# A second token tile scored by rows of the first expert table, and gates spread by one float32 product

## The chip, the cores and the metric

The kernel runs on one core of a Trainium2 chip. The metric is the time of one execution on the device in microseconds (us), the median of several executions. The engines are TensorE (PE in the rows; PEld is its weight load), VectorE (DVE), ScalarE (ACT), GpSimd (POOL) and SyncE (SP). All DMA queues share the core's 16 DMA engines.

## The reference

One layer of a hybrid backbone for 512 tokens of width 2048. Its first half (a state space branch, a pooling branch, a merge) is not touched here. The second half is a product-key expert layer, of which this is the core:

```python
s1, s2 = q[:, :, 0] @ k1.T, q[:, :, 1] @ k2.T         # 8 heads, 128 keys each
v1, i1 = top_k(s1, 16); v2, i2 = top_k(s2, 16)
cand = v1[..., :, None] + v2[..., None, :]            # 16 x 16 pairs
top_s, pos = top_k(cand, 16)                          # 16 experts a head
eid = i1 * 128 + i2                                   # of the pairs chosen
g = softmax(top_s)
act = gelu(einsum('td,thkd->thk', hb, u_tab[eid])) * g
out = einsum('thk,thkd->td', act, v_tab[eid])
```

So each token has 8 x 16 = 128 experts of 16384, each a row of table u (16384 x 2048, float32, 134 MB) that scores it and a row of table v that is added to the output with the weight act.

## The kernel before

The tokens are four tiles of 128 (0 to 3), one token to a partition. The expert layer treats them in two ways.

**By rows.** Tile 0 (`gather_tile`, L1070 to L1110) fetches for each of its 128 experts the 128 rows of u and of v that its tokens ask for, 8 KB each, with an indirect DMA of GpSimd (L1081, 1 MB a transfer, into a pool `rows2` of three buffers). VectorE multiplies the u rows with the tokens and sums (L1096, SCALAR_TENSOR_TENSOR with an accumulator, called the u product below), ScalarE makes the weight (L1097, L1098), and VectorE adds the weighted v rows to the output tile `ffn` (L1089, the v product). A step is one expert: one u product and one v product, the latter for the expert before, then the transfers of this expert's v rows and of the next one's u rows.

**Whole.** Tiles 1 to 3 (`DT`) go through both tables with matmuls. `dense_u` (stage U) scores them against all of u: 128 blocks of 128 experts, and for each two loads of 1024 x 128 weights. `dense_gates` spreads the gates g, 128 a token, over all 16384 experts: for each token a product of two one-hot matrices, one of them weighted. The gates go to memory (`Gd`, by way of a staging tile `ast` with one buffer), the scores too (`Sd`). `dense_v` (stage V) multiplies the two (`weights`, L1193) and runs the result against all of v in 8 passes of 16 blocks, two halves each.

Every weight load, 256 in each stage, is `wload` (L114): SyncE loads 512 KB, ScalarE rounds it to `whi` (L125), and either VectorE or GpSimd makes the remainder `wlo` (L126). `lo_eng` chooses: a share `lo_pool` of them, one in two, goes to GpSimd. `mm3` (L107) then makes each product of three matmuls in rounded float32: high by high, high by low, low by high. There are three buffers of each kind.

What runs beside is spread by `lane`: a list of generators that is stepped `rate` times for each weight load (`tick`). In stage U, lane0 has tile 0's rows at 0.29 steps a load, lane1 the choice of experts (`picks`) and the gates at 1.1. In stage V lane0 goes on at 0.25. Eight blocks before the end of stage U, `late` drains lane1 and makes the first weights. Each engine works in the order in which its instructions stand. In this half GpSimd's order is that of the program, and a scheduler orders the other engines.

Of the kernel before, what the change touches and what calls it, by code (L numbers as in the profile page):

```python
# [93 lines left out]
class Builder:  # L94
# [974 lines left out]

    def gather_tile(self, t, res, acc):  # L1070

        nc, I, V, h2 = self.nc, self.I, self.nc.vector, self.h2[t]
        i1, i2, g = res[t]
        ef = self.keep.tile([P, NK], F32, name=self.nm("ef"))
        V.scalar_tensor_tensor(ef, i1, float(P), i2, op0=OP.mult, op1=OP.add)
        eid = self.keep.tile([P, NK], I32, name=self.nm("eid"))
        V.tensor_copy(eid, ef)

        def row(tab, k):
            r = self.rowp.tile([P, D], F32, tag="row", name=self.nm("row"))  # L1080
            nc.gpsimd.indirect_dma_start(out=r, out_offset=None, in_=I[tab],  # L1081
                                         in_offset=bass.IndirectOffsetOnAxis(ap=eid[:, k:k + 1], axis=0))
            return r
# [312 lines left out]
```

## Time and profile before

| | us |
|---|---|
| median of 3 runs (3973.7 to 3977.77) | 3974.51 |
| the profiled execution | 3968.97 |
| its span, first to last instruction | 3966.9 |
| TensorE busy in the span | 3750.0 (95%) |
| VectorE busy | 2561.8 (65%) |
| GpSimd busy | 1761.6 (44%) |
| ScalarE busy | 1187.9 (30%) |
| stage U, first to last matmul of `psU` | 1586 to 2850 |
| stage V, first to last matmul of `psV` | 2850 to 3947 |

The times below are of the profiled execution, counted from the span's start. A matmul's busy time overlaps its neighbours', so TensorE's pace is read from the distance of starts.

### The profile page before, as it was taken

How to read it: one execution, taken by the hardware profiler on the slowest of the kernel's cores; microseconds unless marked ns; L12 is line 12 of the kernel's file. 1: busy time of each engine (PE TensorE's matmuls, PEld its weight loads, DVE VectorE, ACT ScalarE, POOL GpSimd, SP SyncE). 2: the span in 40 equal slices, each digit the busy share in tenths (PEclk: the TensorE clock that was granted, in tenths of full speed). 3: DMA queues.
4: the chain of work that ended last, by engine and by line, in shares of the span. 5: the costliest groups of instructions: out<-in, count | busy, mean ns of one | idle time of the engine just before them, and what ended most of it. 6: DMA issues, size and time to landing. Idle time of an engine off the chain costs nothing. (4 is left out here: it accounts for less than half of the span.)

```text
span 3966.9 us, 49308 instructions
## 1 busy us (share of the span) xinstructions
PE 3750.0 (95%) x18841; PEld 3196.8 (81%) x18841; DVE 2561.8 (65%) x3331; ACT 1187.9 (30%) x1752; POOL 1761.6 (44%) x997
## 2 busy tenths in 40 slices
PE   5999998889899899899999999999999999999997
PEld 3478876667777778799999999989977887788886
DVE  4364379996563368986767767655666666665664
ACT  4223331112222222333333333323332333333332
POOL 0043115552322323354444444446555666576652
PEclk8999999999999999999999999999999999999999
DMA  8635658789875422477877778778887877887773
GB/s 269 207 124 186 206 166 231 227 227 302 235 233 175 138 70 91 136 263 281 290 272 267 288 273 291 256 289 290 312 300 279 316 285 281 287 318 282 282 277 123
DMA packets 456382, 954.40 MB, mean 241 GB/s; under 512 B 104721, under 2 KB 248465, under 8 KB 421073
## 3 DMA queue, kind: packets, MB, share of 16 engines
q1 hardware_dynamic: 380320, 584.58, 45.5%
q0 software_dynamic: 46464, 301.03, 20.4%
q10 hardware_dynamic: 29360, 65.64, 4.5%
q8 instruction: 147, 2.41, 0.2%
q14 instruction: 91, 0.74, 0.1%
HBM read 859.88 MB, written 94.93 MB: 241 GB/s over the span
## 5 line engine op out<-in xcount | busy, mean ns | idle before, releaser
L125 ACT CAST whi<-wraw 128x1024 fp32r<-128x1024 f32 x712 | 747.2, 1051 | 1825.2 <-PE psU L111 542.1
L126 POOL TENSOR_TENSOR wlo<-wraw,whi 128x1024 fp32r<-128x1024 f32 x284 | 773.4, 2724 | 946.8 <-ACT whi L125 714.4
L126 DVE TENSOR_TENSOR wlo<-wraw,whi 128x1024 fp32r<-128x1024 f32 x428 | 595.7, 1392 | 591.9 <-ACT whi L125 341.8
L112 PE MATMUL psU<-h2Th,wlo 128*128 128x384 f32 x2048 | 693.6, 339 | 31.7 <-DVE wlo L126 20.0
L110 PE MATMUL psU<-h2Th,whi 128*128 128x384 f32 x2048 | 700.4, 342 | 6.5 <-ACT whi L125 6.5
L111 PE MATMUL psU<-h2Tl,whi 128*128 128x384 f32 x2048 | 692.5, 338 | 0.0
L111 PE MATMUL psV<-wlo,ah 128*128 128x512 f32 x1536 | 607.7, 396 | 10.0 <-POOL wlo L126 5.0
L112 PE MATMUL psV<-whi,al 128*128 128x512 f32 x1536 | 607.0, 395 | 0.0
L110 PE MATMUL psV<-whi,ah 128*128 128x512 f32 x1536 | 558.0, 396 | 9.5 <-DVE ffn L1233 5.2
L112 PEld LDWEIGHTS psU<-h2Th,wlo 128*128 128x128 f32 x2048 | 387.2, 189 | 35.9 <-issue 14.2
L1096 DVE SCALAR_TENSOR_TENSOR row<-row,h 128x2048 f32<-128x2048 f32 x128 | 340.9, 2663 | 90.2 <-DMA row<-in_u,eid 90.2
L110 PEld LDWEIGHTS psU<-h2Th,whi 128*128 128x128 f32 x2048 | 389.0, 190 | 8.4 <-ACT whi L125 8.1
L111 PEld LDWEIGHTS psU<-h2Tl,whi 128*128 128x128 f32 x2048 | 388.0, 189 | 0.0
L1089 DVE SCALAR_TENSOR_TENSOR ffn<-row,w,ffn 128x2048 f32<-128x2048 f32 x127 | 357.7, 2816 | 13.5 <-DMA row<-in_v,eid 13.5
L111 PEld LDWEIGHTS psV<-wlo,ah 128*128 128x128 f32 x1536 | 290.8, 189 | 80.7 <-POOL wlo L126 8.2
L110 PEld LDWEIGHTS psV<-whi,ah 128*128 128x128 f32 x1536 | 290.9, 189 | 77.4 <-issue 10.3
L112 PEld LDWEIGHTS psV<-whi,al 128*128 128x128 f32 x1536 | 290.3, 189 | 67.6
L1081 POOL DMA_INDIRECT row<-in_u,eid x128 | 206.2, 1611 | 249.7 <-ACT w L1097 76.6
L1144 DVE TENSOR_TENSOR oh<-io,iT 128x512 bf16<-128x512 bf16 x192 | 168.9, 920 | 193.1 <-PE psd L1152 193.0
L1081 POOL DMA_INDIRECT row<-in_v,eid x128 | 241.0, 1883 | 19.1 <-issue 6.6
L819 DVE SCALAR_TENSOR_TENSOR lacc<-lw,sil,lacc 128x512 f32<-128x512 f32 x240 | 213.6, 890 | 52.1 <-DMA lw<-in_w_mod 50.1
L112 PE MATMUL psg<-hhi,wlo 128*128 128x512 f32 x512 | 205.0, 405 | 25.9 <-DVE wlo L126 25.8
(349 smaller groups left out, 5600.4 us busy)
## 6 DMA issues: line engine op xcount, KB each, us to landing
wraw<-in_uT SPq DMA_DIRECT2D x256, 512.0 KB, 5.2
wraw<-in_v SPq DMA_DIRECT2D x256, 512.0 KB, 6.2
lw<-in_w_mod SPq DMA_DIRECT2D x256, 256.0 KB, 4.3
wraw<-in_w_in SPq DMA_DIRECT2D x96, 512.0 KB, 4.8
wmod<-in_w_mod SPq DMA_DIRECT2D x48, 512.0 KB, 5.1
sd<-sev ACTq DMA_DIRECT2D x64, 384.0 KB, 6.0
gds<-ast ACTq DMA_DIRECT2D x12, 2048.0 KB, 8.8
sr<-sd SPq DMA_DIRECT2D x32, 768.0 KB, 7.2
```

The source lines that it names most:

```text
L110: mm(ps, a.hi, b.hi, start=start, stop=False)
L111: mm(ps, a.hi, b.lo, start=False, stop=False)
L112: mm(ps, a.lo, b.hi, start=False, stop=stop)
L125: nc.scalar.copy(hi, raw)
L126: ins = (eng or nc.vector).tensor_tensor(lo, raw, hi.bitcast(F32), op=OP.subtract)
L819: nc.vector.scalar_tensor_tensor(acc, w, self.sil[:, k, 0:1], acc, op0=OP.mult, op1=OP.add)
L1081: nc.gpsimd.indirect_dma_start(out=r, out_offset=None, in_=I[tab], in_offset=bass.IndirectOffsetOnAxis(ap=eid[:, k:k + 1], axis=0))
L1089: V.scalar_tensor_tensor(acc, v, w, acc, op0=OP.mult, op1=OP.add)
L1096: V.scalar_tensor_tensor(u, u, 1.0, h2, op0=OP.mult, op1=OP.mult, accum_out=w[:, 0:1])
L1144: V.tensor_tensor(oh[:, q], self.io4, iT[:, q, ts].unsqueeze(1).broadcast_to([P, P, NT]), op=OP.is_equal)
```

## The change

Tile 1 is no longer scored by matmul. `dense_u` takes tiles 2 and 3 alone (`DU`), so its matmuls have 256 columns for 384. Tile 1's scores come from gathered u rows (`gather_u`), in stage U on lane0 at 0.64, and end before its gates are spread (lane2, after `gather_u`). Tile 1's gates are multiplied with its scores ahead of the spreading, so `Sd` and the GpSimd product of `weights` hold two tiles. Tile 0's rows, u and v, all move to stage V, at 0.51 steps a load. The share of remainders on GpSimd becomes 0.7 in stage U and 0.62 in stage V. The gates of a token are spread by one product of float32 matrices; before, the gate was three bfloat16 parts and each part a product.

```diff
 DT = (1, 2, 3)
+DU = (2, 3)
+UO = len(DT) - len(DU)
+NU = len(DU) * P
...
-            self.h2 = {0: h2p.tile([P, D], F32, name="h2_0")}
+            self.h2 = {0: h2p.tile([P, D], F32, name="h2_0"), 1: tp.tile([P, D], F32, name="h2_1")}
...
+    def row(self, tab, ids, k):
+        r = self.rowp.tile([P, D], F32, tag="row", name=self.nm("row"))
+        self.nc.gpsimd.indirect_dma_start(out=r, out_offset=None, in_=self.I[tab],
+                                          in_offset=bass.IndirectOffsetOnAxis(ap=ids[:, k:k + 1], axis=0))
+        return r
...
+        self.nc.vector.tensor_copy(eid, ef)
+        return eid
...
+    def gather_u(self, t, res, after):
+
+        nc, V, h2 = self.nc, self.nc.vector, self.h2[t]
+        i1, i2, g = res[t]
+        eid = self.experts(t, res)
+        dots = self.keep.tile([P, NK], F32, name=self.nm("dots"))
+        rows = [self.row("u", eid, k) for k in range(2)]
+        yield
+        for k in range(NK):
+            if k + 2 < NK:
+                rows.append(self.row("u", eid, k + 2))
+            u = rows.pop(0)
+            with self.tc.issue_after(self.last_lo):
+                V.scalar_tensor_tensor(u, u, 1.0, h2, op0=OP.mult, op1=OP.mult, accum_out=dots[:, k:k + 1])
+            yield
+        nc.scalar.activation(dots, dots, AF.Gelu_apprx_tanh)
+        V.tensor_tensor(dots, dots, g, op=OP.mult)
+        res[t] = (i1, i2, dots)
+        after()
...
+    def gather_tile(self, t, res, acc):
+
+        nc, I, V, h2 = self.nc, self.I, self.nc.vector, self.h2[t]
+        g = res[t][2]
+        eid = self.experts(t, res)
+        row = lambda tab, k: self.row(tab, eid, k)
...
-        iT = kp.tile([P, 2, P], BF16, name=self.nm("iT"))
-        nc.scalar.copy(iT, ps[:, 0:2 * P].rearrange("p (j t) -> p j t", j=2))
-        wb = kp.tile([P, 3, P], BF16, name=self.nm("wb"))
-        wf = self.tq.tile([P, P], F32, tag="wf", name=self.nm("wf"))
-        r = self.tq.tile([P, P], F32, tag="wr", name=self.nm("wr"))
-        V.tensor_copy(r, ps[:, 2 * P:3 * P])
-        for q in range(3):
-            V.tensor_copy(wb[:, q], r)
-            if q < 2:
-                V.tensor_copy(wf, wb[:, q])
-                V.tensor_tensor(r, r, wf, op=OP.subtract)
-        ix[t] = (iT, wb)
+        iT = kp.tile([P, 3, P], F32, name=self.nm("iT"))
+        nc.scalar.copy(iT, ps[:, 0:3 * P].rearrange("p (j t) -> p j t", j=3))
+        ix[t] = iT
...
-    def dense_gates(self, ix):
+    def dense_gates(self, ix, ts):
...
-        for j, t in enumerate(DT):
-            iT, wb = ix[t]
+        for t in ts:
+            j, iT = DT.index(t), ix[t]
...
-                    oh = self.ohp.tile([P, 2, P, NT], BF16, tag="oh", name=self.nm("oh"))
-                    for q in range(2):
-                        V.tensor_tensor(oh[:, q], self.io4, iT[:, q, ts].unsqueeze(1).broadcast_to([P, P, NT]), op=OP.is_equal)
-                    R = self.ohp.tile([P, 3, P, NT], BF16, tag="R", name=self.nm("R"))
-                    V.tensor_tensor(R, oh[:, 1].unsqueeze(1).broadcast_to([P, 3, P, NT]),
-                                    wb[:, :, ts].unsqueeze(2).broadcast_to([P, 3, P, NT]), op=OP.mult)
+                    shp = [P, 2, P, NT]
+                    oh = self.ohp.tile(shp, F32, tag="oh", name=self.nm("oh"))
+                    V.tensor_tensor(oh, self.io4.unsqueeze(1).broadcast_to(shp), iT[:, 0:2, ts].unsqueeze(2).broadcast_to(shp),
+                                    op=OP.is_equal)
+                    V.tensor_tensor(oh[:, 1], oh[:, 1], iT[:, 2, ts].unsqueeze(1).broadcast_to([P, P, NT]), op=OP.mult)
                     yield
                     ps = self.psT.tile([P, 512], F32, tag="tr", name=self.nm("psd"))
                     for n in range(NT):
-                        for q in range(3):
-                            nc.tensor.matmul(ps[:, n * P:(n + 1) * P], oh[:, 0, :, n], R[:, q, :, n], start=(q == 0), stop=(q == 2))
+                        nc.tensor.matmul(ps[:, n * P:(n + 1) * P], oh[:, 0, :, n], oh[:, 1, :, n], start=True, stop=True)
                     nc.scalar.copy(st[:, :, t4 * NT:t4 * NT + NT], ps.rearrange("p (t e) -> p e t", t=NT))
                     yield
                 nc.scalar.dma_start(self.Gd[:, j * (P // TG) + tg], st)
...
-                    self.mm3(ps, w[:, kk, :], self.h2T[:, k, DT[0] * P:SEQ], k == 0, k == KT - 1)
+                    self.mm3(ps, w[:, kk, :], self.h2T[:, k, DU[0] * P:SEQ], k == 0, k == KT - 1)
...
-        nc.gpsimd.tensor_tensor(sv, sv, gr, op=OP.mult)
-        self.split(ah, al, sr)
+        no = UO * P // TG
+        nc.gpsimd.tensor_tensor(sv, sv, gr[:, no:], op=OP.mult)
+        first = lambda x: x[:, :, 0:UO * P].rearrange("p i (j t) -> p i j t", t=TG)
+        self.split(first(ah), first(al), gr[:, 0:no].rearrange("p j i t -> p i j t"))
+        self.split(ah[:, :, UO * P:], al[:, :, UO * P:], sr)
         self.A[x] = Split(ah, al)
...
+            def gated():
+                lane2[2].append(late_gates())
+
+            def late_gates():
+                yield from self.dense_keys(1, res, ix)
+                yield from self.dense_gates(ix, DT[:UO])
+
             def prep():
-                yield from self.picks(self.tkp, 0, res)
-                self.lane0[2].append(self.gather_tile(0, res, acc0))
-                for t in DT:
+                yield from self.picks(self.tkp, 1, res)
+                self.lane0[2].append(self.gather_u(1, res, gated))
+                for t in DU:
                     yield from self.picks(self.tkp, t, res)
                     yield from self.dense_keys(t, res, ix)
+                yield from self.picks(self.tkp, 0, res)
                 self.es_t.close()
                 self.stp = es_u.enter_context(pool(name="ast", bufs=1))
-                yield from self.dense_gates(ix)
-
-            self.lane0 = lane0 = self.lane(0.29, [])
-            lane1 = self.lane(1.1, [prep()])
-            self.lo_acc, self.lo_pool = 0.0, 0.5
+                yield from self.dense_gates(ix, DU)
+
+            self.lane0 = lane0 = self.lane(0.64, [])
+            lane1 = self.lane(1.0, [prep()])
+            lane2 = self.lane(1.6, [])
+            self.lo_acc, self.lo_pool = 0.0, 0.7
             es_v = self.es()
             self.raw, self.A = {}, {}
 
             def late():
-                self.drain(lane1)
+                for lane in (lane1, lane0, lane2):
+                    self.drain(lane)
                 es_u.close()
                 self.app, pa = (es_v.enter_context(pool(name=n, bufs=b)) for n, b in (("Ar", 2), ("A0", 1)))
                 self.ahp, self.alp = Turns([pa]), Turns([pa])
...
-            lane0[0], self.lo_pool = 0.25, 0.5
+            lane0, self.lo_pool = self.lane(0.51, [self.gather_tile(0, res, acc0)]), 0.62
             self.dense_v(outs)
             self.drain(lane0)
```

Where the instructions stand now. VectorE in stage U, while gates are spread: `wlo` is a remainder, `oh` and `R` are the one-hot matrices, `row` with `w` or `dots` is a u product, `ffn` a v product. Before:

```order
L126 TENSOR_TENSOR wlo_18404<-wraw_18402,whi_18403 128x1024
L1089 SCALAR_TENSOR_TENSOR ffn_12575<-row_18275,w_18270,ffn_12575 128x2048
L1096 SCALAR_TENSOR_TENSOR row_18277,w_18408<-row_18277,h_0_10626 128x2048
L1144 TENSOR_TENSOR oh_18499<-io_12594,iT_13355 128x512 x2
L1146 TENSOR_TENSOR R_18502<-oh_18499,wb_13357 128x1536
L126 TENSOR_TENSOR wlo_18495<-wraw_18493,whi_18494 128x1024
L1089 SCALAR_TENSOR_TENSOR ffn_12575<-row_18413,w_18408,ffn_12575 128x2048
L1144 TENSOR_TENSOR oh_18590<-io_12594,iT_13355 128x512 x2
```

The same place of the change:

```order
L129 TENSOR_TENSOR wlo_14567<-wraw_14565,whi_14566 128x1024
L1101 SCALAR_TENSOR_TENSOR row_14421,dots_12920<-row_14421,h_1_10627 128x2048
L1167 TENSOR_TENSOR oh_15377<-oh_15377,iT_13109 128x512
L1167 TENSOR_TENSOR oh_15452<-oh_15452,iT_13109 128x512
L1101 SCALAR_TENSOR_TENSOR row_14496,dots_12920<-row_14496,h_1_10627 128x2048
L1165 TENSOR_TENSOR oh_15529<-io_12591,iT_13109 128x1024
L1165 TENSOR_TENSOR oh_15604<-io_12591,iT_13109 128x1024
L129 TENSOR_TENSOR wlo_14684<-wraw_14682,whi_14683 128x1024
```

Between two of VectorE's remainders there stood one step and one group of four tokens' gates; now there stand two u products and two halves of groups, and the remainders on VectorE are three in ten of all.

GpSimd in stage V: `row<-in_v` and `row<-in_u` are the transfers of a step, `wlo` its remainders. Before:

```order
L1081 DMA row_27160<-in_v,eid_12957 128x2048
L1081 DMA row_27162<-in_u,eid_12957 128x2048
L126 TENSOR_TENSOR wlo_27208<-wraw_27206,whi_27207 128x1024
L126 TENSOR_TENSOR wlo_27256<-wraw_27254,whi_27255 128x1024
L1081 DMA row_27265<-in_v,eid_12957 128x2048
L1081 DMA row_27267<-in_u,eid_12957 128x2048
```

Of the change:

```order
L1075 DMA row_26148<-in_v,eid_22145 128x2048
L1075 DMA row_26150<-in_u,eid_22145 128x2048
L129 TENSOR_TENSOR wlo_26196<-wraw_26194,whi_26195 128x1024
L1075 DMA row_26205<-in_v,eid_22145 128x2048
L1075 DMA row_26207<-in_u,eid_22145 128x2048
L129 TENSOR_TENSOR wlo_26253<-wraw_26251,whi_26252 128x1024
```

Two remainders stood between the steps' pairs of transfers, and now one or two.

ScalarE near the end of stage U, where `late` stands: `whi` is a rounding for a weight load, `ah` the rounding of the first weights of stage V, `ast` the copy of a group's gates, `gds<-ast` their transfer to memory. Before (the last `gds<-ast` stands 81 rows ahead of these):

```order
L125 CAST whi_22719<-wraw_22718 128x1024
L125 CAST whi_22774<-wraw_22773 128x1024
L1171 ACTIVATE sev_22685<-psU_22615 128x384
L135 CAST ah_22767<-sr_22759 128x1536
L125 CAST whi_22804<-wraw_22803 128x1024
```

Of the change (six more copies like the first two stand at the "..."):

```order
L128 CAST whi_21635<-wraw_21634 128x1024
L1174 DMA gds<-ast_21120 128x4096
L1172 COPY ast_21472<-psd_21476 128x128x4
L1172 COPY ast_21472<-psd_21485 128x128x4
...
L1174 DMA gds<-ast_21472 128x4096
L138 CAST ah_21563<-gr_21556 128x4x128
L138 CAST ah_21563<-sr_21555 128x4x256
L128 CAST whi_21665<-wraw_21664 128x1024
```

The last gates of tile 1, their transfer, and the first weights, which read them back as `gr`, now stand in one chain ahead of the roundings for the last 13 loads of stage U. On GpSimd the first product `sr` of the weights stands ahead of the remainders of the last 16 loads, in both.

## Rows read from the trace of the kernel before

**Rows 1.** Windows by stage: length, busy (instructions) of PE, PEld, DVE, ACT, POOL, clock, DMA share, GB/s.

```profile
1586.00:2850.00 1264.00, 1225.77 (x7341) 1201.88 (x7340) 882.05 (x841) 411.35 (x637) 607.16 (x272) 0.99 0.75 268
2850.00:3947.00 1097.00, 1077.53 (x4611) 871.02 (x4609) 680.89 (x439) 341.42 (x412) 659.66 (x274) 0.99 0.78 279
```

**Rows 2.** Timeline of PE in four places: start, length, instruction, how many.

```profile
1427.70 0.39 PE L111 MATMUL psq<-h2Tl,whi 128*128 128x512 f32 x1
...
1433.65 0.39 PE L110 MATMUL psq<-h2Th,whi 128*128 128x512 f32 x1
1433.88 1.95 PE L1013 MATMUL pss<-kT,qt 128*128 128x128 f32 x16
...
1998.54 1.59 PE L1152 MATMUL psd<-R,oh 128*128 128x128 bf16 x12
...
2703.24 0.34 PE L110 MATMUL psU<-h2Th,whi 128*128 128x384 f32 x1
...
2711.95 0.34 PE L112 MATMUL psU<-h2Th,wlo 128*128 128x384 f32 x1
```

**Rows 3.** Instructions by tile: count, duration ns min/median/max, first and last start.

```profile
L1013 PEld LDWEIGHTS pss<-kT,qt x128: 187/192/192, 1433.7 to 1595.8; 128*128 128x128 f32 x128
L1013 PE MATMUL pss<-kT,qt x128: 270/275/275, 1433.9 to 1595.9; 128*128 128x128 f32 x128
L126 DVE TENSOR_TENSOR wlo<-wraw,whi x428: 1171/1221/7478, 35.3 to 3931.5; 128x1024 fp32r<-128x1024 f32 x143
L126 POOL TENSOR_TENSOR wlo<-wraw,whi x284: 2337/2412/6053, 1417.4 to 3935.7; 128x1024 fp32r<-128x1024 f32 x142
L1055 DVE TENSOR_TENSOR oh<-oh,iif x8: 2279/2284/4497, 1619.4 to 1704.5; 128x2048 f32<-128x2048 f32 x8
L1199 POOL TENSOR_TENSOR sr<-sr,gr x32: 3479/3518/3692, 2773.8 to 3811.1; 128x1536 f32<-128x1536 f32 x32
L136 DVE TENSOR_TENSOR al<-sr,ah x32: 1745/2436/3222, 2785.3 to 3816.2; 128x1536 fp32r<-128x1536 f32 x32
L1233 DVE TENSOR_TENSOR ffn<-ffn,psV x84: 672/686/689, 3066.0 to 3949.1; 128x512 f32<-128x512 f32 x84
```

**Rows 4.** The same for tile row, in stage V alone, with its DMA landing times.

```profile
L1089 DVE SCALAR_TENSOR_TENSOR ffn<-row,w,ffn x58: 2337/2348/4532, 2860.9 to 3832.3; 128x2048 f32<-128x2048 f32 x58
L1096 DVE SCALAR_TENSOR_TENSOR row<-row,h x57: 2277/2292/4500, 2858.7 to 3819.7; 128x2048 f32<-128x2048 f32 x57
...
DMA to landing us min/median/max: 7.3/9.5/11.9
```

**Rows 5.** Timeline of DVE and of POOL in stage V, around 3108 us.

```profile
3108.07 2.34 DVE L1089 SCALAR_TENSOR_TENSOR ffn<-row,w,ffn 128x2048 f32<-128x2048 f32 x1
3110.34 4.49 DVE L1096 SCALAR_TENSOR_TENSOR row<-row,h 128x2048 f32<-128x2048 f32 x1
...
3108.90 3.78 POOL L126 TENSOR_TENSOR wlo<-wraw,whi 128x1024 fp32r<-128x1024 f32 x1 [3.51 <-ACT whi L125]
```

**Rows 6.** Windows of short stretches, columns as in rows 1.

```profile
1590.00:1710.00 120.00, 95.42 (x534) 92.65 (x533) 117.87 (x204) 36.03 (x51) 53.48 (x19) 0.94 0.50 170
...
3090.00:3150.00 60.00, 60.00 (x261) 48.70 (x260) 47.43 (x30) 21.52 (x26) 45.78 (x18) 1.00 0.97 348
...
3220.00:3240.00 20.00, 20.00 (x88) 16.26 (x87) 12.41 (x7) 8.51 (x9) 16.98 (x7) 1.00 1.03 391
```

**Rows 7.** Timeline of DVE in stage V, steps of tile 0.

```profile
3310.28 4.20 DVE L1089 SCALAR_TENSOR_TENSOR ffn<-row,w,ffn 128x2048 f32<-128x2048 f32 x1 [2.90 <-DMA row<-in_v,eid]
...
3325.69 2.29 DVE L1096 SCALAR_TENSOR_TENSOR row<-row,h 128x2048 f32<-128x2048 f32 x1 [2.03 <-DMA row<-in_u,eid]
...
3327.90 4.48 DVE L1089 SCALAR_TENSOR_TENSOR ffn<-row,w,ffn 128x2048 f32<-128x2048 f32 x1
...
3343.28 2.29 DVE L1096 SCALAR_TENSOR_TENSOR row<-row,h 128x2048 f32<-128x2048 f32 x1 [2.92 <-DMA row<-in_u,eid]
```

**Rows 8.** DMA issues: count, KB each, median us from issue to landing.

```profile
gds<-ast ACTq DMA_DIRECT2D x12, 2048.0 KB, 8.8
...
gr<-gds SPq DMA_DIRECT2D x32, 768.0 KB, 7.9
```

More of the change, by code (lines that the diff above doesn't have):

```diff
@@ L977, in tail @@
                 for t in range(TT):
-                    h2 = self.h2[0][:, cs] if t == 0 else bp.tile([P, 512], F32, tag="h2", name=self.nm("h2"), bufs=3)
+                    h2 = self.h2[t][:, cs] if t in self.h2 else bp.tile([P, 512], F32, tag="h2", name=self.nm("h2"), bufs=3)
                     nc.vector.scalar_tensor_tensor(h2, x1[:, t, cs], rs[:, 2, t:t + 1], sh2[:, cs], op0=OP.mult, op1=OP.add)
@@ L1068, in picks, with experts @@
         yield
+    def row(self, tab, ids, k):
[3 more added lines that the diff above has]
+        return r
+    def experts(self, t, res):
+        i1, i2, g = res[t]
+        ef = self.keep.tile([P, NK], F32, name=self.nm("ef"))
+        self.nc.vector.scalar_tensor_tensor(ef, i1, float(P), i2, op0=OP.mult, op1=OP.add)
+        eid = self.keep.tile([P, NK], I32, name=self.nm("eid"))
+        self.nc.vector.tensor_copy(eid, ef)
+        return eid
+    def gather_u(self, t, res, after):
+        nc, V, h2 = self.nc, self.nc.vector, self.h2[t]
+        i1, i2, g = res[t]
+        eid = self.experts(t, res)
[13 more added lines that the diff above has]
+        after()
     def gather_tile(self, t, res, acc):
         nc, I, V, h2 = self.nc, self.I, self.nc.vector, self.h2[t]
[L1073 to L1083, printed above, removed]
+        g = res[t][2]
+        eid = self.experts(t, res)
+        row = lambda tab, k: self.row(tab, eid, k)
         def vacc(k, v, w):
@@ L1113, in dense_keys @@
     def dense_keys(self, t, res, ix):
-        nc, V, kp = self.nc, self.nc.vector, self.keep
+        nc, kp = self.nc, self.keep
         ps = self.psT.tile([P, 512], F32, tag="tr", name=self.nm("pst"))
@@ L1162, in dense_u @@
                 late()
-            ps = self.psA.tile([P, 512], F32, tag="acc", name=self.nm("psU"))[:, 0:ND * P]
+            ps = self.psA.tile([P, 512], F32, tag="acc", name=self.nm("psU"))[:, 0:NU]
             for kh in range(2):
@@ L1167, in dense_u @@
                     k = kh * 8 + kk
-                    self.mm3(ps, w[:, kk, :], self.h2T[:, k, DT[0] * P:SEQ], k == 0, k == KT - 1)
+                    self.mm3(ps, w[:, kk, :], self.h2T[:, k, DU[0] * P:SEQ], k == 0, k == KT - 1)
             if i2 % 2 == 0:
-                ev = self.evp.tile([P, 2, ND * P], F32, tag="sev", name=self.nm("sev"))
+                ev = self.evp.tile([P, 2, NU], F32, tag="sev", name=self.nm("sev"))
             nc.scalar.activation(ev[:, i2 % 2], ps, AF.Gelu_apprx_tanh)
@@ L1186, in weights_load @@
         i2, j2 = slice(x * 4, x * 4 + 4), slice(x * 4 % NC, x * 4 % NC + 4)
-        sr = self.app.tile([P, 4, ND * P], F32, tag="sr", name=self.nm("sr"))
+        sr = self.app.tile([P, 4, NU], F32, tag="sr", name=self.nm("sr"))
         gr = self.app.tile([P, ND * P // TG, 4, TG], F32, tag="gr", name=self.nm("gr"))
@@ L1261, in peer @@
         pool = lambda **k: tc.tile_pool(**k)
-        self.Sd = [self.dram.tile([P, NC, ND * P], F32, name=f"sd{c}") for c in range(P // NC)]
+        self.Sd = [self.dram.tile([P, NC, NU], F32, name=f"sd{c}") for c in range(P // NC)]
         self.Gd = self.dram.tile([P, ND * P // TG, P, TG], F32, name="gds")
```

2 lines of the change are left out of this document (1 added, 1 removed).

## The prediction, made before the changed kernel ran

> **What bounds the kernel now.** I read the windows by stage first, then TensorE's timeline for its pace, then single instructions for their prices, and last the places where engines wait for one another.
>
> The windows by stage [rows 1] show TensorE busy for 1225.8 of 1264 us in stage U and for 1077.5 of 1097 in stage V: it bounds both, and VectorE, GpSimd and the DMA share (0.75 and 0.78) have room. The pace is read from starts [rows 2]: fifty matmuls of 384 columns take 2711.95 - 2703.24 = 8.71 us, 0.174 each; twenty-six of 512 columns 5.95 us, 0.229 each. The line through both has a slope of 0.427 ns a column, so one of 256 columns is estimated at 0.120 us. Stage U has 128 x 16 x 3 = 6144 matmuls, 1070 us, and 96 `psd` groups of 12 bfloat16 matmuls in bursts of 1.59 us [rows 2], 153 us at most: 1223 of 1264 are explained. Stage V has 4608 x 0.229 = 1055 of 1097.
>
> What the table of stages hides is in the timeline around 3108 us [rows 5]. A v product of VectorE began at 3108.07; GpSimd's remainder began during it and took 3.78 us, where 2.41 is its median [rows 3]. Then the u product, begun while GpSimd worked, took 4.49, where 2.29 is its median [rows 4]. Whoever starts first goes on at its own speed, and the other's record grows by about what is left. So I treat VectorE operations with two inputs in SBUF, and GpSimd's TENSOR_TENSOR, as users of one port, and add their undisturbed times. The Trainium skill says the same of this pair ("SBUF — State Buffer", section "SBUF: two separate sides"): the shared port pair is an exclusive lock, held for the whole instruction by whoever takes it first; by that rule the sums below hold in full, and the trace agrees with 3.78 and 4.49.
>
> Stage V's port sum before, by [rows 3, 4]: VectorE 127 remainders x 1.221 = 155, 57 u products x 2.29 = 131, 58 v products x 2.35 = 136, 31 `al` x 1.745 = 54; GpSimd 128 remainders x 2.412 = 309, 31 `sr` x 3.518 = 109. That is 894 of 1097 us, 81%, so it is hidden.
>
> **The change, part by part.**
>
> *TensorE in stage U.* 6144 x 0.120 = 735. A float32 matmul of 128 columns is two instructions: the 16 `pss` took 1.95 us [rows 2], less the last one's 0.275 over 15, so 0.112 each, and a group of four tokens 0.9; 96 groups are 86 us. Together 821 for 1223, so up to 402 us are offered. Their weight loads are recorded at 192 ns [rows 3], yet follow each other every 112, so I let weight loads bound nothing.
>
> *The port in stage U.* VectorE: 0.3 x 256 = 77 remainders, 94; 128 u products, 293; for each of 96 groups one comparison of 1024 elements, taken at the price of the remainder's 1024, 117, and one product of 512, taken at the 0.69 of the 512-element add, 66; the picks' 16 products of 2.284, 37: 607. GpSimd: 179 remainders x 2.412 = 432. Sum 1039, of which some 38 are in the last 16 loads. So 1000 for the first 240 loads, where TensorE wants 770: the port is the new bound. How full can it get? At the start of stage U [rows 6], from 1590 to 1710, VectorE was recorded busy for 117.87 of 120 us, 98%, and TensorE gave way there. On the other side, from 3090 to 3150 the port work that stands there (8 remainders and 4 each of u products, v products and `al` on VectorE, 7 remainders and 3 `sr` on GpSimd) adds up to 62.8 in 60 us, a factor of 0.955. I take the former, since there the port was what was waited for: 1000/0.98 = 1020.
>
> *The end of stage U.* Tile 1's gates end last, and `late` drains them ahead of the first weights. ScalarE's order puts in one row: a transfer of gates, 8.8 us [rows 8]; eight copies of the next group, about a microsecond each, which wait for that transfer since `ast` has one buffer; its transfer, 8.8; the loading of `gr`, 7.9; the `sr` product, 3.518 x 2/3 = 2.35; and a remainder on GpSimd behind it, 2.41. These are 38 us, with nothing behind them that feeds TensorE: three buffers hold three loads. Before, the gates were done long ahead of this point, so it cost nothing. I take 37 (22 if the first transfer is hidden, 48 if the copies wait their turn). The last 16 loads then go at TensorE's pace, 16 x 24 x 0.120 = 46.
>
> Stage U: 1020 + 37 + 46 = 1103 for 1264, a gain of 161.
>
> *Stage V.* TensorE's work is the same. Port: 97 remainders on VectorE, 118; 128 u products, 293; 128 v products, 301; `al` in two pieces, 1.9 x 32 = 61; GpSimd 159 remainders, 384; `sr` 31 x 2.35 = 73: 1230 for 894, now above TensorE's 1097. At 98%: 1255; at 0.955: 1175. The adds from PSUM (0.686) I leave out of it.
>
> *Bytes in stage V.* Rows 256 x 1.05 = 268 MB, table v 134, `sr` 17, `gr` 25, some 8 more: 450 MB, where 279 x 1097 = 306 went before [rows 1]. The busiest stretches [rows 6] moved 348 GB/s over 60 us at a share of 0.97, and 391 over 20 us at 1.03. So 450 MB want 1151 to 1293 us, about what the port wants. The Trainium skill ("DMA: Bandwidth & Descriptors", section "Specifications") gives a core some 358 GB/s of HBM; by that the stage would be 1257 us, an estimate, and the 391 of one stretch is above it.
>
> *The rows' chain in stage V.* With three buffers the u rows of step k+1 are asked for when the v product of step k-1 has ended. [Rows 7] give that distance: from 3314.48 (3310.28 + 4.20) to 3325.69 and from 3332.38 to 3343.28, 11.2 and 10.9 us, of which landing is 7.3 to 11.9 [rows 4]. Two steps are then at least 11.0 + 2.29 + 2.35 = 15.6, and with both products held up by GpSimd (4.5 each) and a remainder between 21.3: 7.8 to 10.65 us a step, 1000 to 1363 for 128. Stage V at today's length would want 8.6.
>
> Three limits stand close, at 1255, 1151 to 1293, and 1000 to 1363. I take the port's 1255 and add 25 for waits that the other two cause, 0.2 us a step: 1280, a loss of 183.
>
> *Sum.* The part ahead of stage U is not touched, 1586, and the tail of 20 stays. 1586 + 1103 + 1280 + 20 = 3989 for a span of 3966.9. The profiled execution lies 2.1 above its span and the median 5.5 above that: 3989 + 7.5 = 3996.5, so **3996**. A difference under 0.2%, 8 us, is about what a measurement of this kernel can't tell from none.
>
> **The rivals.**
>
> *Faster.* The port lets more overlap than I count, as in the stretch at 3090 us, and the DMA engines keep the rate of the stretch at 3220. Then stage U is 955 + 37 + 46 = 1038 and stage V 1175 + 15 = 1190: 1586 + 1038 + 1190 + 20 + 7.5 = 3842. For it: TensorE lost nothing in that stretch, so the port may not have been full. Against it: the held-up products [rows 5]. It decides from a stage V of 1258 us on down (2361, today's sum of both stages, less 1103).
>
> *Rows come later.* With the DMA engines full all through stage V, each landing moves from the median 9.5 to today's maximum 11.9. Two steps are then 21.3 + 2.4 = 23.7, and 128 are 1517: 4233. For it: asked-for bytes of 410 GB/s at TensorE's pace, above every row. Against it: rates sink with the pace, so the queue does not grow without end.
>
> *The change does not speed up the matmuls.* If weight loads at 192 ns do bound matmuls of 256 columns, stage U wants 6144 x 0.192 + 86 = 1266 and 37: 4196. Against it: the `pss` pitch.
>
> TensorE's clock is 0.99 in both stages, and 0.94 where it starved from 1590 to 1710 [rows 1, 6]. It would have to sink to 1055/1280 = 0.82 of itself in stage V before it bounded, so it is no rival.
>
> **How the numbers follow.** My forecast holds with 0.55; its own range is 3930 to 4080 (stage U 22 to 48 us of gap, stage V 1222 to 1363), of which 0.14 is faster, 0.07 within 0.2%, 0.34 slower. The faster rival has 0.30 (0.28, 0.01, 0.01), later rows 0.11 and weight loads 0.04, all slower. Together: faster 0.42, within 0.2% 0.08, slower 0.50. The range of 8 in 10 reaches past 3842 and short of 4233: 3810 to 4200.
>
> **What would show it.** Right: a pitch of 0.12 us in `psU`; stage U some 1100 long with VectorE and GpSimd busy nearly throughout, and a hole of about 37 us in TensorE ahead of the last 16 loads; in stage V steps about 10 us apart, products of 4.5 us nearly as common as those of 2.3, a DMA share of 0.95 or more, TensorE waiting for `wlo`. Wrong: TensorE without waits in stage V (the port overlaps), landing times well over 12 us (later rows), a `psU` pitch near 0.19, or no hole before stage V.

## The result and the profile after

The median is **4229.66 us** (4 runs, 4214.59 to 4232.12); the kernel before, beside it, took 3974.11. The ratio is 1.0636, with a 95% interval of 1.0609 to 1.0664: 6.4% slower. The forecast was 3996 (3810 to 4200), a change of half a per cent. The direction was right, though the forecast gave it a chance of 0.50 only, so that is no merit; the size was not, and the time lies outside the range.

The profiled execution has a span of 4230.3 us, 241 more than the 3989 of the sum. Windows of the changed kernel by stage (columns as in [rows 1]); stage U runs to the first `psV`, stage V to the last:

```profile
1586.00:2804.00 1218.00, 1011.59 (x7032) 985.82 (x7031) 874.36 (x789) 375.32 (x501) 757.75 (x310) 0.91 0.73 260
2804.00:4201.00 1397.00, 1167.99 (x4609) 911.70 (x4608) 1011.00 (x642) 371.18 (x579) 957.60 (x447) 0.92 0.88 319
```

| | before | forecast | after |
|---|---|---|---|
| stage U, from 1586 to the first `psV` | 1264 | 1103 | 1218 |
| stage V, first to last `psV` | 1097 | 1280 | 1397 |
| tail | 20 | 20 | 29 |

So the excess of 241 us over the sum is 115 in stage U, 117 in stage V and 9 in the tail. Neither TensorE (84% busy in stage V) nor VectorE (72%), GpSimd (69%) or the DMA engines (0.88) is full there. That is the puzzle: no one limit shows.

TensorE's timeline in stage U, at a group of gates, and at the end of the stage:

```profile
2001.16 0.28 PE L113 MATMUL psU<-h2Th,whi 128*128 128x256 f32 x1
...
2003.54 0.28 PE L113 MATMUL psU<-h2Th,whi 128*128 128x256 f32 x1
...
2003.78 2.13 PE L1171 MATMUL psd<-oh 128*128 128x128 f32 x8
2005.56 0.46 PE L115 MATMUL psU<-h2Th,wlo 128*128 128x256 f32 x1
...
2734.56 4.09 PE L1171 MATMUL psd<-oh 128*128 128x128 f32 x16 [0.26 <-DVE oh L1167]
2758.39 0.58 PE L115 MATMUL psU<-h2Th,wlo 128*128 128x256 f32 x1 [19.73 <-POOL wlo L129]
```

From 2001.16 to 2003.54 there are 21 matmuls of 256 columns: 0.113 us each, where 0.120 was forecast. A group of four tokens' gates, though, takes 2005.56 - 2003.78 = 1.78 us, and not 0.9. The hole before stage V is there as described: no matmul of `psU` starts between 2720.28 and 2758.39. ScalarE's rows show its parts, 6.44 us for the first transfer of gates, the copies, and 13.73 us until the last gates are read back:

```profile
2725.19 1.07 ACT L1172 COPY ast<-psd 128x512 f32<-128x512 f32 x2 [6.44 <-DMA gds<-ast]
...
2753.01 0.62 ACT L138 CAST ah<-gr 128x512 fp32r<-128x512 f32 x1 [13.73 <-DMA gr<-gds]
```

In stage V, waits by engine and what was waited for (us in total, times, longest), from 2804 to 4202:

```profile
ACT whi L128 <- DMA wraw<-in_v: 331.3, 112, 9.4
...
POOL row L1075 <- DVE ffn L1119: 260.7, 91, 7.1
...
PE psV L114 <- POOL wlo L129: 208.8, 77, 10.2
ACT whi L128 <- PE psV L115: 189.7, 49, 8.2
...
POOL row L1075 <- DVE row L1126: 77.4, 27, 4.3
```

GpSimd's transfers of rows waited 338 us for VectorE's products (the buffers), and nearly all of TensorE's waits are for remainders that GpSimd makes. Timelines of four engines show how the two are tied, around 3310 us:

```profile
3302.52 0.62 ACT L138 CAST ah<-gr 128x512 fp32r<-128x512 f32 x1 [5.00 <-PE psV L114]
...
3303.17 0.69 DVE L139 TENSOR_TENSOR al<-gr,ah 128x512 fp32r<-128x512 f32 x1 [7.14 <-ACT ah L138]
3303.78 2.35 DVE L1119 SCALAR_TENSOR_TENSOR ffn<-row,w,ffn 128x2048 f32<-128x2048 f32 x1
...
3306.39 2.75 POOL L1075 DMA_INDIRECT row<-in_u,eid  x1 [7.06 <-DVE ffn L1119]
3309.17 2.35 POOL L1219 TENSOR_TENSOR sr<-sr,gr 128x1024 f32<-128x1024 f32 x1
3311.47 4.68 POOL L129 TENSOR_TENSOR wlo<-wraw,whi 128x1024 fp32r<-128x1024 f32 x2
...
3313.87 0.80 PE L114 MATMUL psV<-wlo,ah 128*128 128x512 f32 x1 [5.41 <-POOL wlo L129]
3314.47 0.63 PE L115 MATMUL psV<-whi,al 128*128 128x512 f32 x1
```

Read it from the top. ScalarE's rounding `ah` waits for TensorE; VectorE waits for it with `al`, and behind `al` stands a v product. GpSimd stands 7.06 us at a transfer of rows whose buffer that product frees. Behind the transfer stand `sr` and two remainders, and TensorE waits 5.41 us for the first of these. Then its matmuls start 0.43 us apart for a while, at a granted clock of 0.50 from 3314.4 to 3318, the lower of the two clocks (1.2 GHz). Counted from all starts in the trace, 365 of the 4607 distances in stage V lie between 0.35 and 0.6 us, 161 us in all and some 77 more than at the usual 0.229; before, there were 34. Every engine waits for another, and none is the bound by itself.

### The profile page after: what moved, and what is told of

Its sections match the earlier page's. It is cut to its first block, busy times and chain, and to the rows that moved or that the text cites. A ratio compares the mean times of both kernels' runs of the same rounds, so it can differ in the third digit from the quotient of the medians.

```text
span 4230.3 us, 49042 instructions
## 1 busy us (share of the span) xinstructions
PE 3615.2 (85%) x18457; PEld 3013.1 (71%) x18457; DVE 2880.0 (68%) x3421; ACT 1180.7 (28%) x1785; POOL 2205.3 (52%) x1206
## 4 chain that ended last, share of the span: by engine, by line
DMA 16%; PE 16%; POOL 14%; issue 12%; DVE 7%; ACT 1%; POOLq 0%; ACTq 0%; DVEq 0%
DMA row<-in_v,eid 11%; POOL wlo L129 8%; POOL row L1075 5%; PE psd L1171 3%; DMA wraw<-in_uT 3%; PE psU L115 3%; PE psU L113 2%; PE psU L114 2%; DMA wraw<-in_v 2%; DVE row L1101 2%; PE psq L113 1%; PE psq L115 1%; PE psq L114 1%; POOL sr L1219 1%; DVE wlo L129 1%
## 5 line engine op out<-in xcount | busy, mean ns | idle before, releaser
L129 POOL TENSOR_TENSOR wlo<-wraw,whi 128x1024 fp32r<-128x1024 f32 x365 | 991.0, 2722 | 487.8 <-ACT whi L128 306.7
L129 DVE TENSOR_TENSOR wlo<-wraw,whi 128x1024 fp32r<-128x1024 f32 x347 | 508.8, 1466 | 524.7 <-ACT whi L128 280.3
L114 PE MATMUL psV<-wlo,ah 128*128 128x512 f32 x1536 | 655.8, 427 | 210.4 <-POOL wlo L129 208.8
L115 PE MATMUL psU<-h2Th,wlo 128*128 128x256 f32 x2048 | 607.2, 298 | 134.4 <-POOL wlo L129 115.7
L1075 POOL DMA_INDIRECT row<-in_u,eid x256 | 488.4, 1908 | 367.7 <-DVE ffn L1119 260.7
L113 PE MATMUL psU<-h2Th,whi 128*128 128x256 f32 x2048 | 605.2, 296 | 23.7 <-ACT whi L128 23.7
L114 PE MATMUL psU<-h2Tl,whi 128*128 128x256 f32 x2048 | 596.2, 291 | 0.0
L113 PE MATMUL psV<-whi,ah 128*128 128x512 f32 x1536 | 464.2, 399 | 18.6 <-DVE ffn L1255 9.3
L1101 DVE SCALAR_TENSOR_TENSOR row<-row,h 128x2048 f32<-128x2048 f32 x128 | 380.4, 2980 | 62.8 <-DMA row<-in_u,eid 62.7
L1119 DVE SCALAR_TENSOR_TENSOR ffn<-row,w,ffn 128x2048 f32<-128x2048 f32 x127 | 334.7, 2635 | 102.7 <-DMA row<-in_v,eid 80.5
L1126 DVE SCALAR_TENSOR_TENSOR row<-row,h 128x2048 f32<-128x2048 f32 x128 | 354.8, 2772 | 28.8 <-DMA row<-in_u,eid 28.5
L1171 PE MATMUL psd<-oh 128*128 128x128 f32 x768 | 204.6, 426 | 40.3 <-DVE oh L1167 31.1
```

The source lines that it names most:

```text
L113: mm(ps, a.hi, b.hi, start=start, stop=False)
L114: mm(ps, a.hi, b.lo, start=False, stop=False)
L115: mm(ps, a.lo, b.hi, start=False, stop=stop)
L129: ins = (eng or nc.vector).tensor_tensor(lo, raw, hi.bitcast(F32), op=OP.subtract)
L1075: self.nc.gpsimd.indirect_dma_start(out=r, out_offset=None, in_=self.I[tab], in_offset=bass.IndirectOffsetOnAxis(ap=ids[:, k:k + 1], axis=0))
L1101: V.scalar_tensor_tensor(u, u, 1.0, h2, op0=OP.mult, op1=OP.mult, accum_out=dots[:, k:k + 1])
```

## The experiments

A scheduler orders all engines but GpSimd anew for each kernel, so a stage that an edit doesn't touch can move too: stage U of three kernels with the same stage U took 1218, 1207, 1203 and, with only small tiles moved, 1206. Stage V of `gates_bf16` below, which has the changed kernel's stage V, took 1388 for 1397. So 15 us in stage U and 10 in stage V are no finding. Stage V is read from one row of each kernel, the high by high matmuls of `psV` with their first and last start.

**Port, transfers, or both?** There are three theories of what sets stage V: (1) VectorE's and GpSimd's port time; (2) the chain of the rows and GpSimd's queue; (3) the bytes.

`v_resident`: the rows of stage V stay where they are.

```diff
-        row = lambda tab, k: self.row(tab, eid, k)
+        still = {tab: self.row(tab, eid, 0) for tab in ("u", "v")}
+        spare = self.rowp.tile([P, D], F32, tag="row", name=self.nm("spare"))
+        row = lambda tab, k: still[tab]
...
-                V.scalar_tensor_tensor(u, u, 1.0, h2, op0=OP.mult, op1=OP.mult, accum_out=w[:, 0:1])
+                V.scalar_tensor_tensor(spare, u, 1.0, h2, op0=OP.mult, op1=OP.mult, accum_out=w[:, 0:1])
```

> Leaves out: in stage V, all transfers of rows but two; every step multiplies the same two resident rows (u product into a spare tile), so its output is not the layer's. Products, remainders and their port time (1230 us by the sum of the prediction) stay. Changed kernel: stage V 1398 us, span 4230. If the port sets stage V (theory 1), it stays near 1398, 1340 to 1400. If the rows' chain sets it - GpSimd's queue, where a transfer waits for a row buffer and for VectorE's port ahead of the remainders (theory 2) - or the bytes (theory 3), it falls to what port or TensorE allow: 1100 to 1260, total 3940 to 4100.

`v_narrow`: its products are narrow.

```diff
-                V.scalar_tensor_tensor(acc, v, w, acc, op0=OP.mult, op1=OP.add)
+                V.scalar_tensor_tensor(acc[:, 0:64], v[:, 0:64], w, acc[:, 0:64], op0=OP.mult, op1=OP.add)
...
-                V.scalar_tensor_tensor(u, u, 1.0, h2, op0=OP.mult, op1=OP.mult, accum_out=w[:, 0:1])
+                n = slice(0, 64)
+                V.scalar_tensor_tensor(u[:, n], u[:, n], 1.0, h2[:, n], op0=OP.mult, op1=OP.mult, accum_out=w[:, 0:1])
```

> Leaves out: the products of tile 0's rows in stage V are made for 64 of 2048 columns, so the output is wrong there; all transfers stay (450 MB). Port sum 1230 - 594 = 640 us. If bytes set stage V (theory 3; 319 GB/s at a share of 0.88 in the changed kernel) it stays near 1398. If the port does (theory 1), TensorE bounds it: 1060 to 1120. If the rows' chain does (theory 2), two steps are 11 us of landing and little else, 5.5 us a step, and with the buffers free early the remainders no longer wait: 1060 to 1180, unless landing grows.

Measured: 4093.4 and 4064.0 us. The row of `psV`, and the window of stage V, of `v_resident`:

```profile
L113 PE MATMUL psV<-whi,ah x1536: 387/393/796, 2792.8 to 4062.5; 128*128 128x512 f32 x192
```

```profile
2793.00:4063.00 1270.00, 1126.82 (x4607) 894.33 (x4606) 1137.20 (x646) 369.53 (x581) 657.59 (x193) 0.94 0.45 141
```

and of `v_narrow`:

```profile
L113 PE MATMUL psV<-whi,ah x1536: 387/393/796, 2789.3 to 4037.5; 128*128 128x512 f32 x192
```

```profile
2789.00:4038.00 1249.00, 1121.66 (x4613) 887.74 (x4611) 427.97 (x646) 374.21 (x582) 730.62 (x447) 0.96 0.94 357
```

with these waits among those from 2850 to 3800 (us in total, times, longest):

```profile
POOL row L1075 <- DVE row L1127: 147.4, 56, 13.6
POOL row L1075 <- DVE ffn L1119: 106.9, 45, 8.8
...
PE psV L114 <- POOL wlo L129: 76.1, 31, 7.2
```

No theory alone survives: 1270 is just above the range that theories 2 and 3 gave the first run, and 1248 fits none in the second. Without transfers the port's 1230 take 1270 us, with VectorE busy for 90%: the prediction's 1255, nearly. With the transfers and hardly any products it takes 1248, at 357 GB/s and a DMA share of 0.94: inside the prediction's 1151 to 1293 for the bytes. The Trainium skill ("DMA: Bandwidth & Descriptors", section "Specifications") puts a core's HBM limit near 358 GB/s. This trace lies beside that with 357, but the next run moved 366, so no run here shows it as a ceiling. Nor is 1248 the time of the bytes alone: the waits above show GpSimd's transfers still waiting for buffers and TensorE for remainders behind them, and `lo_dve` below passes about the same bytes in 1208. Each load by itself fits its forecast; together they make 1397. A part of the difference is seen in a row of each kernel: with wide products (changed kernel, from 2804 on) issuing a transfer of u rows takes GpSimd 1.72 us, with narrow ones 0.95. The columns are count and ns min/median/max; first the changed kernel, then `v_narrow`:

```profile
L1075 POOL DMA_INDIRECT row<-in_u,eid x128: 942/1724/3022, 2810.6 to 4177.1; - x128
```

```profile
L1075 POOL DMA_INDIRECT row<-in_u,eid x127: 940/946/1997, 2800.9 to 4013.7; - x127
```

So VectorE's products hold up the issue as well. For 256 transfers that is some 200 us of GpSimd's time (0.78 x 256), on top of the 0.95 us that each takes anyway; the prediction had nothing for either. The Trainium skill has a rule of this kind ("SBUF — State Buffer", section "SBUF: two separate sides"): while VectorE runs an operation of a two-port mode, GpSimd is locked out of the shared port pair and can't write the descriptors of its own transfers. Here the issue grows beside products of two SBUF inputs, which that rule does not name; what in the issue waits is not shown.

`lo_dve`: all remainders on VectorE.

```diff
-            self.lo_acc, self.lo_pool = 0.0, 0.7
+            self.lo_acc, self.lo_pool = 0.0, 0.0
...
-            lane0, self.lo_pool = self.lane(0.51, [self.gather_tile(0, res, acc0)]), 0.62
+            lane0, self.lo_pool = self.lane(0.51, [self.gather_tile(0, res, acc0)]), 0.0
```

> All remainders on VectorE in both stages (shares 0.7 and 0.62 become 0). Port sums: stage U 313 + 607 - 94 = 826 us for 1039, stage V 313 + 293 + 301 + 61 + 73 = 1041 for 1230. GpSimd keeps the transfers and sr. Theory 1 (port): stage U 1218 falls to about 1000, stage V 1398 to 1100 to 1180, total 3700 to 3800. Theory 2 (GpSimd's queue): stage V also falls, since no remainder stands behind a waiting transfer, but the chain of 11 us landings with longer VectorE queues leaves 1150 to 1300. Theory 3 (bytes): stage V stays at 1330 to 1400.

Measured: 3924.6 us, a ratio of 0.9908 (0.9891 to 0.9924) to before. Its row and its window of stage V:

```profile
L113 PE MATMUL psV<-whi,ah x1536: 387/393/796, 2664.4 to 3872.5; 128*128 128x512 f32 x192
```

```profile
2664.00:3875.00 1211.00, 1115.14 (x4606) 875.14 (x4607) 1040.09 (x794) 375.48 (x577) 481.32 (x287) 0.98 0.96 366
```

Stage U 1078 for 1218, stage V 1208 for 1397: two constants undo the whole loss, and more. The gain is smaller than theory 1 wanted (1000 for stage U, 1180 at most for stage V), and stage V lies within theory 2's 1150 to 1300; theory 3's 1330 to 1400 is refuted. At a DMA share of 0.96 the bytes are now the likeliest bound of stage V; no run settles it.

**The float32 gates.** `gates_alone` is the kernel before with only the change in `dense_keys` and `dense_gates`; `gates_bf16` is the changed kernel with these two as before.

> The kernel before, with the gates spread by one float32 product alone. In the changed kernel a group of 8 float32 instructions took 2.13 us against 1.59 for 12 bfloat16 before, and TensorE bounds stage U of before. So +0.4 to +0.55 us a group, 96 groups: 38 to 53 us slower, 4010 to 4030. The rule of the prediction (0.9 us a group) would give 50 us faster, about 3925.

> The changed kernel with the gates spread by three bfloat16 products as before (one part of the change undone). In the kernel before, the float32 gates alone cost 41 us where TensorE bounds. If TensorE's 1.8 us a group for 1.4 counts in the changed kernel's stage U too: 1218 falls by 30 to 60 us, most of it in the loads with gates (98, 93 and 87 us for 16) and in the drained end (86). If the port alone sets stage U, VectorE's work of a group is the same (0.42 x 2 + 0.96 = 1.80 for 1.91): 0 to 15 us. Stage V as it was.

Their rows of `psV`, whose first start ends stage U:

```profile
L110 PE MATMUL psV<-whi,ah x1536: 387/393/628, 2890.4 to 3981.3; 128*128 128x512 f32 x192
```

```profile
L113 PE MATMUL psV<-whi,ah x1536: 387/393/795, 2773.2 to 4161.0; 128*128 128x512 f32 x192
```

Measured: `gates_alone` 4004.6 us, 1.0110 (1.0092 to 1.0128): stage U 1304 for 1264, as expected by the 2.13 of the trace. `gates_bf16` 4192.8 us, 1.0565 (1.0546 to 1.0585): stage U 1187 for 1218, 31 us less, at the lower end of what was expected if TensorE counts. Against the other kernels with that stage U (1203 to 1207) it is 16 to 20 us, hardly above the 15 that are no finding. So by itself the float32 product costs some 40 us where TensorE bounds, and 16 to 31 where it does not; it paid in none of these kernels. (With all remainders on VectorE it is 35 us, 3924.6 against 3889.3 below, in two batches.)

**What ties the two limits?** `v_bufs4` gives stage V a fourth buffer of rows.

```diff
...
+            rp = es_v.enter_context(pool(name="rows3", bufs=1))
+            self.rowp = Turns([self.rowp] * 3 + [rp] * 1)
```

> The changed kernel with four row buffers in stage V for three (the index tiles of the gates move to a pool of stage U to make room). So far: without transfers stage V is 1270 us, without products 1249, with both 1397. If the 130 us between come from the ring of buffers (a transfer waits in GpSimd's queue for a product, remainders behind it; theory 2), a fourth buffer takes a good part of the 338 us of waits in GpSimd's queue: stage V 1290 to 1340. If port and bytes hold each other up without the buffers, it stays at 1375 to 1400.

Measured: 4176.7 us; the row of stage V:

```profile
L113 PE MATMUL psV<-whi,ah x1536: 387/393/796, 2792.1 to 4146.9; 128*128 128x512 f32 x192
```

1355: 42 us less, and outside both expectations. The buffers are a part, but a small one. (The lines left out move the index tiles of the gates, as the expectation says.) The next two kernels each hold one test for either stage. In stage V both put half as many remainders on GpSimd (0.31 for 0.62), the second with four buffers. In stage U `u_resident` keeps its rows in place (as `v_resident` did) and `u_narrow` makes narrow products.

> Two edits, one in each stage of the changed kernel. Stage U leaves out all transfers of rows but two (the same two resident rows are scored every time, so the scores are wrong): port sum 1039 as it was, 132 MB less. If the port sets stage U it stays at 1180 to 1218; if GpSimd's queue of transfers or the bytes do, it falls to 1060 to 1130. Stage V has 0.31 of the remainders on GpSimd for 0.62: port sum 216 + 293 + 301 + 61 + 191 + 73 = 1135, bytes as they were. If the larger limit alone counted, stage V would be the bytes' 1249; if limits add to one another, about half way between 1397 (port sum 1230) and 1211 (1041): 1290 to 1320.

> Two edits again. Stage U makes tile 1's u products for 64 of 2048 columns (scores wrong), all transfers stay: port sum 1039 - 293 = 746. If the port sets stage U, 940 to 1020, near TensorE's 735 + 171 and the hole; if bytes, 1150 to 1218. Stage V has four row buffers and 0.31 of the remainders on GpSimd: between 1355 (four buffers, port 1230) and 1211: 1270 to 1290, or 1249 if the bytes alone are left.

Measured: 4061.1 and 4071.9 us. The rows of `psV`, first of `u_resident`, then of `u_narrow`:

```profile
L113 PE MATMUL psV<-whi,ah x1536: 387/393/797, 2685.6 to 4022.1; 128*128 128x512 f32 x192
```

```profile
L113 PE MATMUL psV<-whi,ah x1536: 387/393/796, 2744.6 to 4036.8; 128*128 128x512 f32 x192
```

Stage V: 1337 and 1292. That makes a table of two by two:

| stage V, us | three buffers | four buffers |
|---|---|---|
| port sum 1230, 0.62 on GpSimd | 1397 | 1355 |
| port sum 1135, 0.31 on GpSimd | 1337 | 1292 |

A buffer gives 42 or 45 us, half of GpSimd's remainders 60 or 63: they add. A maximum of limits, which would give 1250 to 1270 in every cell, is refuted. Both of the lower cells came out above their ranges (1290 to 1320 and 1270 to 1290). Stage U took 1100 without transfers and 1159 with narrow products, for 1218. The first lies in the range for GpSimd's queue or the bytes (1060 to 1130), the second just inside that for the bytes (1150 to 1218); both speak against port time alone, though the DMA share was only 0.80 with narrow products (1600 to 2600). And 1100 without transfers is what the prediction had for the stage with them.

Moving remainders off GpSimd does two things, though: it lowers the port time, and it takes them out of GpSimd's queue. `lo_twice` parts these: every remainder that GpSimd had is made twice on VectorE (`twice` is set for the loads that `lo_eng` would have given to GpSimd).

```diff
...
             ins = (eng or nc.vector).tensor_tensor(lo, raw, hi.bitcast(F32), op=OP.subtract)
             if eng in (None, nc.vector):
                 self.last_lo = ins.ins
+            if twice:
+                self.last_lo = nc.vector.tensor_tensor(lo, raw, hi.bitcast(F32), op=OP.subtract).ins
...
```

> The changed kernel with all remainders on VectorE, and those that stood on GpSimd (0.7 and 0.62 of them) made twice there, into the same tile. Port sums: stage U 826 + 179 x 1.22 = 1045, stage V 1041 + 159 x 1.22 = 1235, both within 6 us of the changed kernel's 1039 and 1230; bytes and transfers the same; but GpSimd has no remainders standing behind transfers that wait. If GpSimd's queue is what couples port and bytes (theory 2), stage V is 1255 to 1290 for 1397 and stage U 1060 to 1130 for 1218. If port time and bytes add to one another by themselves, they stay near 1397 and 1218 (1350 to 1400, 1180 to 1218).

Measured: 4110.8 us. Its row, its window of stage V, and of its waits there (2800 to 4000) the largest of GpSimd and of TensorE's matmuls:

```profile
L113 PE MATMUL psV<-whi,ah x1536: 387/393/796, 2762.9 to 4077.4; 128*128 128x512 f32 x192
```

```profile
2763.00:4080.00 1317.00, 1158.25 (x4607) 900.26 (x4608) 1226.42 (x962) 373.11 (x581) 518.68 (x287) 0.94 0.92 339
```

```profile
POOL row L1077 <- DVE ffn L1121: 444.9, 112, 10.0
...
PE psV L114 <- DVE wlo L133: 102.4, 57, 5.8
```

Stage V is 1315 for 1397, at the same sum of port times, bytes and buffers: 82 us went when the remainders left GpSimd's queue. One other thing changed, that their port time now lies on one engine instead of two; `v_resident`, where two engines share the port without transfers, leaves at most 40 us for that (1270 less 1230). GpSimd's transfers wait even longer than in the changed kernel (445 us for the v products alone, for 261), and no remainder stands behind them. The other 60 us above the port's 1255 stay. VectorE is busy for 93% here, since on its own it now has those 1235 less the 73 of `sr`, and some 60 of adds from PSUM: it is nearly the bound itself, which the sum by ports did not show. Neither expectation for stage V (1255 to 1290, 1350 to 1400) was met; it came out between them. Stage U: 1177, 41 less, just under the range for port and bytes that add; what else holds it up was not found.

**A version that is faster than both.** `lo_dve_bf16` is `lo_dve` with the gates of `gates_bf16`; `best1` starts tile 0's rows at the end of stage U; `best2` adds a fourth buffer. `before_lo_dve` is the kernel before with its share of 0.5 on GpSimd set to 0, in both stages.

```diff
...
                 lane2[2].append(late_gates())
+                lane3[2].append(self.gather_tile(0, res, acc0))
...
+            lane3 = self.lane(0.5, [])
...
-            lane0, self.lo_pool = self.lane(0.51, [self.gather_tile(0, res, acc0)]), 0.0
+            lane0, self.lo_pool = lane3, 0.0
+            lane0[0] = 0.43
```

> All remainders on VectorE (3924.6 us with float32 gates) and bfloat16 gates. With the port relieved TensorE is nearer to bounding stage U (906 of 1078): 20 to 50 us less, 3875 to 3905.

> As the run before it, and tile 0's rows begin in stage U, at 0.5 steps a load behind the last step of tile 1's rows, and go on in stage V at 0.43. Stage V moved 368 GB/s at a share of 0.97 with the remainders on VectorE, stage U 296 at 0.81. If bytes set stage V there, some 25 steps of 2.1 MB less are 50 MB, 140 us of 368 GB/s, at most down to TensorE's 1080 or so: stage V 1090 to 1140 for 1211; stage U may lose 0 to 40. Total 3790 to 3870. If VectorE's own work (1041 us of port time and the waits) sets it, stage V falls by a fifth of the products, 60 us or less, and stage U grows by as much: no gain.

> All remainders on VectorE, bfloat16 gates, tile 0's rows from the end of stage U on, and four row buffers in stage V. Three buffers gave 1180 for stage V at a DMA share of 0.95, 461 us of transfers waiting for the v product. If those waits cost, stage V falls to 1130 to 1160 and the total to 3835 to 3870; if bytes (354 GB/s) are the limit it stays within 10 us of 1180 and of 3888.

> The kernel before, with all remainders on VectorE in both stages. TensorE bounds it at 95%; its port sum falls by a fifth (stage V 894 to 740). If moving the remainders pays by itself, 20 to 40 us less (3930 to 3950); if it pays only where port and bytes compete, within 10 us of before.

Their rows of `psV`, in this order:

```profile
L113 PE MATMUL psV<-whi,ah x1536: 387/393/796, 2643.1 to 3848.3; 128*128 128x512 f32 x192
L113 PE MATMUL psV<-whi,ah x1536: 387/393/797, 2676.8 to 3856.8; 128*128 128x512 f32 x192
L113 PE MATMUL psV<-whi,ah x1536: 387/393/796, 2693.5 to 3901.8; 128*128 128x512 f32 x192
L110 PE MATMUL psV<-whi,ah x1536: 387/393/628, 2835.8 to 3928.5; 128*128 128x512 f32 x192
```

| | us | ratio to before (95%) | stage U | stage V |
|---|---|---|---|---|
| `lo_dve_bf16` | 3889.3 | 0.9788 (0.9765 to 0.9810) | 1057 | 1205 |
| `best1` | 3888.4 | 0.9805 (0.9785 to 0.9824) | 1091 | 1180 |
| `best2` | 3921.0 | 0.9886 (0.9864 to 0.9908) | 1107 | 1208 |
| `before_lo_dve` | 3951.1 | 0.9965 (0.9952 to 0.9979) | 1250 | 1093 |

The first came as expected. `best1` came as the second of its expectations had it, that of no gain: what it took from stage V (25 us, not 70 or more) it gave back in stage U (34). `best2` missed both: the fourth buffer, with no remainders behind the transfers, did not help, and why it made stage V longer by 28 us was not followed up. The last, 16 us less, lies between its two ranges. It shows that moving the remainders is worth only 0.35% where TensorE bounds, so most of the gain of `lo_dve_bf16` is the second tile by rows, once the port is not overdrawn.

## Why the prediction was wrong

**The pace and the hole: right.** The matmuls of `psU` started 0.113 us apart, where 0.120 was forecast. The last 16 loads of stage U began at 2718 and took 86 us, hole included, for 37 + 46 = 83. That hole is in TensorE's rows above: gates drained up to 2738, then 19.73 us without work.

**The float32 gates: wrong price.** I read the `pss` row as two instructions a matmul at 0.112 us and priced a group at 0.9; it takes 1.78, two instructions a matmul at 0.22. That price was outside anything that I allowed. Its worth in stage U is 16 to 31 us of the excess of 115.

**The step that failed** is the last one of stage V: "Three limits stand close, at 1255, 1151 to 1293, and 1000 to 1363. I take the port's 1255 and add 25 for waits that the other two cause". The runs showed 1270 for the port without transfers, and 1208 to 1248 with the bytes and a lighter port, so the limits were right; the addition is 142, not 25. Of these 142, 82 went when the remainders left GpSimd's queue (`lo_twice`), where they stood behind transfers that wait for a buffer. How much of that the slow issue beside VectorE's products adds was not tried. I had the pieces: the 7 to 11 us of each landing, the two remainders between transfers in GpSimd's order. I used the chain only for its own length, and did not ask who stands behind the waiting transfer. The other 60 stay open. VectorE's own adds and TensorE's slow restarts (in `lo_twice` still 305 slow distances, some 68 us above the usual pace) may make them up, and so may the bytes, at a DMA share of 0.92; none of these was tried by itself. Of the signs that I had asked for, a DMA share of 0.95 or more in stage V did not come (0.88), nor were VectorE and GpSimd busy nearly throughout stage U (874 and 758 of 1218 us).

**The same omission in stage U**: "1000/0.98 = 1020" had no term for transfers at all. Without them the stage is 1100, against 1103 forecast with them; with them 1218. That 1100 and 1103 agree so well is in part luck, since the 1100 holds the float32 gates at their true price. Of those 118 us the order of GpSimd's queue explains at most 41 (`lo_twice`), and 77 stay open, as do the 15 us by which the first `psU` came late (1600.8).

**The port as exclusive: borne out.** `v_resident`, with nothing else in the way, needs 1270 for a sum of 1230. The Trainium skill's rule of the lock ("SBUF — State Buffer", section "SBUF: two separate sides") agrees with that number. The faster rival's overlap of 0.955 did not come.

**The rivals.** *Rows come later* gave 4233, 4 us from the median, by luck: it forecast stage U at 1103 and stage V at 1517, where they are 1218 and 1397, and VectorE's products waited only 80.5 + 28.5 us for rows in stage V. *Weight loads* that bound are refuted by the pitch. And the clock, set aside as no rival since it would have had to fall to 0.82, stood at 0.92: it did not bound, but the slow restarts above took some 77 us more than at the usual pace, for which no rival had a term.

## What to carry to other kernels

Where two resources are each loaded to about the stage's length, don't forecast the larger of the two: ask which in-order queue both pass through, and what stands behind the instruction that waits in it. An instruction that may wait long (a transfer into a ring of buffers) should not share a queue with one that feeds the bounding engine; here, moving that work to the other engine was worth 190 us of stage V, of which 82 remained when its port time was held equal. And an engine that makes the same tile at half the speed (2.41 us for 1.22 here), through the same port, is no help once that port is what is scarce.

## What the runs showed of the hardware

An indirect transfer's issue on GpSimd took 0.95 us beside narrow products of VectorE, and a median of 1.72 beside wide ones: the issue is held up by VectorE as GpSimd's own arithmetic is. It is not products alone: sorted by the VectorE instruction that each issue of the changed kernel's stage V overlapped longest, the median is 0.95 us with none (40 issues), 0.96 beside an add from PSUM (13), 1.77 beside a remainder (29) and 2.75 beside a u product (93). A float32 matmul of 128 columns ran as two instructions of some 0.22 us each in `psd` (1.78 us for 8), where the sixteen `pss` of [rows 2] had been 0.112 apart. Both are float32; the operands of `psd` are every fourth element of the one-hot tile, those of `pss` lie together. Whether that is the reason was not tried.
